# A decoder layer on one core: weights earlier, gate work on GpSimd, another order of side steps, and the 64-to-128 merge in two fours

## The chip, the cores and the metric

The kernel runs on one core of a Trainium2 chip. The time is what the device takes for one execution, in microseconds; the median of the runs counts. The engines are PE (TensorE, matrix products), DVE (VectorE), ACT (ScalarE), POOL (GpSimd) and SP (SyncE, which issues the DMAs here). Each engine works off its own instructions in order, and waits for others by semaphores.

## The reference

One layer on x of 256 x 2048 (float32), with two branches side by side:

```python
shift, scale, gate = split(silu(c) @ w_ada + b_ada)
h = rms_norm(x, norm_pre_w) * (1 + scale) + shift
proj = h @ w_in                    # all branch inputs and the two merge gates
q, k, v = conv_silu(gdn_qkv)       # 16 q/k heads, 32 value heads, width 128
o_a = gated_delta_rule(l2(q), l2(k), v, g_log, beta)     # needs (I + lower)^-1 for each head
y_a = (rms_norm(o_a) * silu(gdn_z)) @ w_proj_gdn
h_b = mlstm(conv_silu(ml_qk), ml_v, i, f)                # 8 heads
y_b = (sigmoid(ml_o) * rms_norm(h_b) * silu(ml_z)) @ w_proj_mlstm
x + gate * rms_norm((sigmoid(gate_a) * y_a + sigmoid(gate_b) * y_b) @ w_out)
```

## The kernel before

Every large product is made of three products of split operands: a weight tile `raw` (128 x 2048, 1 MB) is loaded by SP, ACT rounds it to `whi`, DVE or POOL subtracts to get `wlo` (in halves of 1024 columns, "pieces" below; four buffers each, three of `raw`), and PE multiplies both with `h_hi` and `h_lo`. `Stream` runs these pieces: it prepares up to three pieces ahead of the one that PE uses. `split_w` deals the subtraction out between POOL and DVE by a share (`START_SHARE`, then `LAST_SHARE` in the last start block, then 0).

Stages: the conditioning products with `ar` tiles (`ada`, DVE) run beside the first blocks of the start, in which 14 groups of 512 output columns (`START`: gates and value inputs) are summed over 16 chunks of `h` in blocks of chunks (`BLOCKS`); `part` holds the sums. Then eight GDN periods, `gdn_period(zg)`: each streams the projections of an even pair of heads, of z, and of an odd pair, and the work on the heads runs as "side" generators that advance by one step for each half piece or piece of the stream: `gdn_stage1` for each pair (convolution, SP's load `gb` of the decay rows, POOL's mask `dd`, ACT's exponentials, products `psa`, `psb`, `psv`), then for the four heads `base_inverse` (32 x 32 blocks are inverted on DVE in `xx`, whose input comes through DRAM by `ud` and `ug` and whose result goes back by `xd` and `xcmp`), then `gdn_stage2` (the blocks are merged: `mp` and `mx` from 32 to 64, `mq` and `mz` from 64 to 128; then `pa`, `pb`, `pc`, `po`), and the output transposes `pt<-con,on` with ACT's copies `oT`. Then the mLSTM heads in the same manner, and the projections `py` and `pw`.

What sets the order is the program: steps of the generators are written between pieces of the stream. `Side` keeps a `debt` of DVE's extra work; each step pays off `STEP_US`, and `room` holds a generator back while the debt is high. `banks` and `free` hold it back until PSUM tiles are free. What one engine gets is then in its queue in that order, DMAs on SP included.

```python
def step(self):
    self.t += 1
    self.debt = max(0.0, self.debt - STEP_US)
    for e in list(self.gens):
        if next(e[1], self) is self:
            self.gens.remove(e)
```

Of the kernel before, what the change touches and what calls it, by code (L numbers as in the profile page):

```python
# [25 lines left out]
LAST_SHARE = 0.3  # L26
STEP_US = 2.1
# [90 lines left out]
def hybrid_layer_kernel(  # L118
# [150 lines left out]
    crow = sp.tile([P, D], F32, name="crow", tag="ar", bufs=ADA_BUFS)[0:1]  # L269
    SP.dma_start(crow, c_row)  # L270
# [5 lines left out]
    A.activation(crow, crow, AF.Silu)  # L276
    for q in range(4):
        T.matmul(csil[:, q * 512:(q + 1) * 512], one_row, crow[:, q * 512:(q + 1) * 512], start=True, stop=True)
# [28 lines left out]
    def x_chunks(k0, k1):  # L307

        x_scale(k0)
        for k in range(k0, k1, 2):  # L310
            if k + 2 < k1:
                x_scale(k + 2)
            x_turn(k)
    x_chunks(0, 6)
# [10 lines left out]
    def h_chunk(k):  # L325
# [6 lines left out]
        split(hf, h_hi[:, k], h_lo[:, k], G)  # L332
# [11 lines left out]
    def ada_units():  # L344

        adders = []
        for k in range(KC):
            for pt in range(2):
                def prep(h, raw, k=k, pt=pt):
                    V.scalar_tensor_tensor(raw, raw, 1.0, csil, op0=ALU.mult, op1=ALU.mult,  # L350
                                           accum_out=ad[:, pt * KC + k:pt * KC + k + 1])
                    if 4 <= 2 * k + pt < 8:
                        j = 2 * (2 * k + pt)
                        if j > 8:
                            x_turn(j)
                        if j < 14:
                            x_scale(j + 2)
                    h_chunks(k - 1)
                    if pt == 1:
                        due.append(k)  # L360
                        if k == 0:
                            h_chunks(0)
                            x_chunks(6, 10)
                        elif k == KC - 1:
                            banks_open()
# [7 lines left out]
    def banks_open():  # L373

        nonlocal pg
        pcs.close()
        pg = ctx.enter_context(tc.tile_pool(name="pg", bufs=4, space=PSUM))
        share[1] = LAST_SHARE

    def branches_open():  # L380
# [3 lines left out]
        share[1] = 0.0  # L384
# [8 lines left out]
    def add_start_groups(bi):  # L393
        k0, nk = BLOCKS[bi]
        lastb = bi == len(BLOCKS) - 1
        adders, parts_ = [], []
        for g in range(len(START)):
            st_ = {}

            def use(h, hi, lo, g=g, st_=st_):  # L400
                if h == 0:
                    st_["ps"] = [jtile(f"pn{i}") for i in range(2)]
                for kc in range(min(2, nk - 2 * h)):
                    kr = h * 2 + kc
                    k = k0 + kr
                    h_chunks(k)
                    o = kc * 512
                    for b in range(2):
                        mm3(st_["ps"][b], h_hi[:, k, b * P:(b + 1) * P], h_lo[:, k, b * P:(b + 1) * P],
                            hi[:, o:o + 512], lo[:, o:o + 512], kr == 0, kr == nk - 1)  # L410

            def after(g=g, st_=st_):
                for b in range(2):
                    if bi == 0:
                        A.copy(part[g][:, b], st_["ps"][b])
                    else:
                        V.tensor_tensor(part[g][:, b], st_["ps"][b], part[g][:, b], op=ALU.add)  # L417
                if bi == len(BLOCKS) - 2 and g == 3:
                    late_consts()
                if lastb:  # L420
                    pt = part[g].rearrange("p b c -> p (b c)")
                    A.activation(pt, pt, AF.Silu if g in (9, 11, 13) else AF.Sigmoid)
                    if g < 8:
                        SP.dma_start(gate_dr[g], part[g])
                    elif g % 2:
                        V.tensor_tensor(part[g], part[g], part[g - 1], op=ALU.mult)
                        SP.dma_start(gate_dr[8 + (g - 8) // 2], part[g])
                    if g == NG - 1:
                        branches_open()
            parts_.append((w_in[START[g]][:, k0 * 512:(k0 + nk) * 512], use, after))  # L430
        if nk == 2:
            for g in range(0, NG, 2):
                def use2(h, hi, lo, g=g):
                    parts_[g + h][1](0, hi, lo)
                    parts_[g + h][2]()
                adders.append(lambda g=g, use2=use2:
                              stream.add((parts_[g][0], parts_[g + 1][0]), prep_w, use2))
        else:
            for src, use, after in parts_:
                adders.append(lambda src=src, use=use, after=after:  # L440
                              stream.add(src, lambda h, raw: prep_w(h, raw, nk * 512), use, (nk + 1) // 2, after))
# [3 lines left out]
    def gates(ps):  # L445
# [15 lines left out]
        V.tensor_scalar(u, e, 1.0, None, op0=ALU.add)  # L461
# [4 lines left out]
        V.tensor_scalar(u, u, -1.0, None, op0=ALU.add)  # L466
        V.tensor_tensor(e, e, u, op=ALU.subtract)
        V.tensor_tensor(e, e, r, op=ALU.mult)
        V.tensor_tensor(l, l, e, op=ALU.add)
        mn, sp_ = ab, u  # L470
        V.scalar_tensor_tensor(mn, xb, 0.0, l, op0=ALU.min, op1=ALU.subtract)
        V.scalar_tensor_tensor(sp_, xb, 0.0, l, op0=ALU.max, op1=ALU.add)
# [865 lines left out]
```

## Time and profile before

| | us |
|---|---|
| median of 3 runs (1624.42 to 1629.12) | 1628.48 |
| the profiled execution | 1630.52 |
| its span | 1628.7 |
| PE busy | 1589.6 |
| DVE, ACT, POOL busy | 1130.8, 935.9, 266.2 |

The granted clock of PE was 0.998 on average, and the DMAs moved 372.37 MB. In the lines shown below, L223 is the line of all split products, L169 and L170 those of the rounding and the subtraction, so tiles are told apart by name. The number in brackets at a row's end is idle time before the instruction, with what ended it.

### The profile page before, as it was taken

The page shows a single profiled execution, that of the slowest core. Times are in us where ns is not written, and L with a number is a line of the kernel's source. Part 1 is how long each engine was busy: PE and PEld are TensorE (multiplying, and loading weights), DVE is VectorE, ACT ScalarE, POOL GpSimd, SP SyncE. Part 2 cuts the span into 40 slices and gives each one's busy share as a digit, 9 for nine tenths or more (in the row PEclk, how much of TensorE's full clock was granted, in tenths as well). Part 3 has the DMA queues.
Part 4 walks back from the last instruction along what each step waited for, and adds up shares of the span by engine and source line. Part 5 has one row for each costly group of instructions (what it writes and reads, how often), then busy time and mean ns, then how long its engine had stood idle before and what let it go on. Part 6 is the DMA issues. An engine that isn't in the chain of part 4 may idle for free.

```text
span 1628.7 us, 25437 instructions
## 1 busy us (share of the span) xinstructions
PE 1589.6 (98%) x9844; PEld 1388.5 (85%) x9844; DVE 1130.8 (69%) x1784; ACT 935.9 (57%) x1494; POOL 266.2 (16%) x200
## 2 busy tenths in 40 slices
PE   6999999999999999999999999999999999999998
PEld 4888888789998999999898989789987788888886
DVE  5586555665678797969696969686777556756654
ACT  7744446564655666666666666665565544444442
POOL 3877762220000010000000000000100000100100
PEclk9999999999999999999999999999999999999999
DMA  9998775665455555555546464657888668766573
GB/s 375 381 363 327 274 280 181 240 246 206 163 182 166 181 178 191 173 177 173 183 164 196 162 198 168 185 177 257 289 312 303 211 236 298 275 239 245 201 271 118
DMA packets 96259, 372.37 MB, mean 229 GB/s; under 512 B 26261, under 2 KB 46213, under 8 KB 58249
## 3 DMA queue, kind: packets, MB, share of 16 engines
q1 hardware_dynamic: 96138, 370.75, 64.8%
q8 instruction: 77, 1.26, 0.3%
q14 instruction: 44, 0.36, 0.1%
HBM read 354.40 MB, written 16.31 MB: 228 GB/s over the span
## 4 chain that ended last, share of the span: by engine, by line
PE 66%; DVE 7%; ACT 4%; DMA 3%; issue 2%; POOL 1%; SPq 0%; DVEq 0%; POOLq 0%; ACTq 0%
PE pt L223 24%; PE py L223 15%; PE pn L223 14%; PE pw L223 5%; DVE wlo L170 3%; ACT whi L169 2%; DMA raw<-in_dram 1%; DMA ya<-o_dr 1%; PE psa L223 1%; DVE mqk L579 1%; DVE part L417 1%; DVE gacc L1034 1%; PE mq L777 1%; PE mz L785 1%; PE pt L859 0%
## 5 line engine op out<-in xcount | busy, mean ns | idle before, releaser
L170 DVE TENSOR_TENSOR wlo<-raw,whi 128x1024 fp32r<-128x1024 f32 x439 | 545.1, 1250 | 267.6 <-ACT whi L169 261.7
L169 ACT CAST whi<-raw 128x1024 fp32r<-128x1024 f32 x514 | 531.2, 1051 | 301.7 <-PE pn L223 142.9
L223 PE MATMUL pt<-h_hi,whi 128*128 128x256 f32 x1280 | 368.2, 288 | 0.2 <-ACT sz L877 0.2
L223 PE MATMUL pt<-h_hi,wlo 128*128 128x256 f32 x1280 | 362.4, 283 | 1.5 <-DVE wlo L170 1.5
L223 PE MATMUL pt<-h_lo,whi 128*128 128x256 f32 x1280 | 362.0, 283 | 0.0
L223 PE MATMUL pn<-whi,h_hi 128*128 128x512 f32 x896 | 353.9, 395 | 3.7 <-ACT whi L169 2.9
L223 PE MATMUL pn<-wlo,h_hi 128*128 128x512 f32 x896 | 351.0, 392 | 5.4 <-POOL wlo L170 4.1
L223 PE MATMUL pn<-whi,h_lo 128*128 128x512 f32 x896 | 350.2, 391 | 0.0
L223 PEld LDWEIGHTS pt<-h_hi,wlo 128*128 128x128 f32 x1280 | 245.1, 192 | 2.1 <-DVE wlo L170 2.1
L223 PEld LDWEIGHTS pt<-h_hi,whi 128*128 128x128 f32 x1280 | 245.3, 192 | 1.7 <-ACT sz L877 0.4
L223 PEld LDWEIGHTS pt<-h_lo,whi 128*128 128x128 f32 x1280 | 245.3, 192 | 0.2
L223 PEld LDWEIGHTS pn<-wlo,h_hi 128*128 128x128 f32 x896 | 168.8, 188 | 43.4 <-POOL wlo L170 6.6
L223 PEld LDWEIGHTS pn<-whi,h_hi 128*128 128x128 f32 x896 | 168.7, 188 | 40.3 <-ACT whi L169 3.3
L170 POOL TENSOR_TENSOR wlo<-raw,whi 128x1024 fp32r<-128x1024 f32 x75 | 180.4, 2413 | 126.1 <-ACT whi L169 113.0
L223 PEld LDWEIGHTS pn<-whi,h_lo 128*128 128x128 f32 x896 | 168.7, 188 | 35.7 <-POOL h_lo L170 0.3
L223 PE MATMUL py<-whi,yhi 128*128 128x512 f32 x384 | 150.9, 393 | 2.8 <-ACT vt L965 2.8
L223 PE MATMUL py<-whi,ylo 128*128 128x512 f32 x384 | 149.8, 390 | 0.0
L223 PE MATMUL py<-wlo,yhi 128*128 128x512 f32 x384 | 149.7, 390 | 0.0
L417 DVE TENSOR_TENSOR part<-pn,part 128x512 f32<-128x512 f32 x112 | 74.0, 686 | 50.5 <-PE pn L223 50.5
L169 ACT CAST yhi<-ya 128x512 fp32r<-128x512 f32 x48 | 29.9, 622 | 129.9 <-PE py L223 125.6
L170 DVE TENSOR_TENSOR ylo<-ya,yhi 128x512 fp32r<-128x512 f32 x48 | 33.2, 692 | 94.1 <-ACT yhi L169 92.2
L579 DVE SCALAR_TENSOR_TENSOR qs<-pt,gcv,qs 128x255 f32<-128x255 f32 (+2 forms) x192 | 92.1, 480 | 4.6
(242 smaller groups left out, 1787.7 us busy)
## 6 DMA issues: line engine op xcount, KB each, us to landing
raw<-in_dram SPq DMA_DIRECT2D x259, 1024.0 KB
ar<-in_dram SPq DMA_DIRECT2D x32, 1024.0 KB
raw<-in_dram SPq DMA_DIRECT2D x28, 512.0 KB
ya<-o_dr SPq DMA_DIRECT2D x32, 256.0 KB
gate_dr<-part SPq DMA_DIRECT2D x11, 512.0 KB
gb<-rows SPq DMA_DIRECT2D x20, 256.0 KB
ug<-ud SPq DMA_DIRECT2D x32, 128.0 KB
o_dr<-oT SPq DMA_DIRECT2D x16, 256.0 KB
```

Source lines behind the costliest of these rows:

```text
L169: A.copy(hi, src)
L170: (eng or V).tensor_tensor(lo, src, hi.bitcast(F32), op=ALU.subtract)
L223: T.matmul(ps, l, r, start=start and i == 0, stop=stop and i == 2, skip_group_check=True)
L417: V.tensor_tensor(part[g][:, b], st_["ps"][b], part[g][:, b], op=ALU.add)
L579: V.scalar_tensor_tensor(dst[:, n, sh:], src[:, 0:S - sh], taps(n, 3 - sh), dst[:, n, sh:], op0=ALU.mult, op1=ALU.add)
L777: T.matmul(psp[64:128, m * 64:(m + 1) * 64], um(m)[0:64, 64:128], y0[:, m], start=True, stop=True)
L785: T.matmul(psz[0:64, m * 64:(m + 1) * 64], p2[64:128, m], x0[64:128, m, 64:128], start=True, stop=True)
L1034: V.scalar_tensor_tensor(gate_half[q], raw[:, q * 1024:(q + 1) * 1024], sil[:, i:i + 1], gate_half[q], op0=ALU.mult, op1=ALU.add)
```

## The change

It alters the following. The conditioning vector is loaded into two `part` tiles, so that the first weights follow two `ar` loads; the start blocks become seven, in which the first six groups begin with one chunk, and the stream prepares one piece ahead in the first of them. The gate arithmetic goes from DVE to POOL with more steps between, POOL also multiplies the gate parts, and the share of POOL in the last start block becomes 0. The step budget goes from 2.1 to 1.6 us, and the steps that hold PE long take something off the debt. The start of `gdn_stage2` is tied to a step count. The output transposes wait for four free tiles instead of two. In the mLSTM heads mask and exponentials are issued within the convolution, and the scores wait for the seventh GDN application. In the merge from 64 to 128, eight `mq` and eight `mz` become four first products, then four second products in turn with the other four first ones, then the last four second ones, all in one PSUM tile `mqz`.

```diff
-LAST_SHARE = 0.3
-STEP_US = 2.1
+STAGE2_STEPS = 32
+STEP_US = 1.6
...
-    crow = sp.tile([P, D], F32, name="crow", tag="ar", bufs=ADA_BUFS)[0:1]
-    SP.dma_start(crow, c_row)
+    crow = [part[4 + i].rearrange("p b c -> p (b c)")[0:1] for i in range(2)]
+    for i in range(2):
+        SP.dma_start(crow[i], c_row[:, i * 1024:(i + 1) * 1024])
...
-    stream = Stream(load_w, side)
-    BLOCKS = ((0, 2), (2, 2), (4, 4), (8, 4), (12, 4))
-    PACE = (4, 9.5, 16.5, 26, 32, 32)
+    stream = Stream(load_w, side, 2)
+    NG, NE = len(START), 6
+    EARLY, REST, ALL = range(NE), range(NE, NG), range(NG)
+    BLOCKS = ((EARLY, 0, 1, 1.1, 3.5), (REST, 0, 2, 4, 8), (EARLY, 1, 3, 8, 12), (REST, 2, 2, 12, 16.5),
+              (ALL, 4, 4, 16.5, 26), (ALL, 8, 4, 26, 32), (ALL, 12, 4, 32, 32))
...
-        share[1] = LAST_SHARE
+        share[1] = 0.0
...
+                stream.ahead = 3 if bi else 1
...
-                        V.tensor_tensor(part[g], part[g], part[g - 1], op=ALU.mult)
+                    G.tensor_tensor(part[g], part[g], part[g - 1], op=ALU.mult)
...
-        V.tensor_scalar(u, e, 1.0, None, op0=ALU.add)
+        G.tensor_scalar(u, e, 1.0, None, op0=ALU.add)
...
+        res["t"] = side.t
         psa = gtile("psa", True)
...
+        side.debt -= 1.6
...
-        yield from wait(1)
+        yield
+        while zg < 7 and side.t < res["t"] + STAGE2_STEPS - 1:
+            yield
         side.add(gdn_stage2(zg, res, zr), 0)
...
-        psp = gtile("mq", True)
-        for m in range(8):
-            T.matmul(psp[64:128, m * 64:(m + 1) * 64], um(m)[0:64, 64:128], y0[:, m], start=True, stop=True)
...
-        psz = gtile("mz", True)
-        for m in range(8):
-            T.matmul(psz[0:64, m * 64:(m + 1) * 64], p2[64:128, m], x0[64:128, m, 64:128], start=True, stop=True)
...
+        psq = psz = gtile("mqz", True)
...
+        for i in range(3):
+            side.debt -= 0.5
+            first, second = slice(4 * i, 4 * i + 4), slice(4 * i - 4, 4 * i)
+            for m in range(4 * i, 4 * i + 4):
+                if i > 0:
+                    T.matmul(psz[0:64, (m - 4) * 64:(m - 3) * 64], p2[64:128, m - 4], x0[64:128, m - 4, 64:128],
+                             start=True, stop=True)
+                if i < 2:
+                    T.matmul(psq[64:128, m * 64:(m + 1) * 64], um(m)[0:64, 64:128], y0[:, m], start=True, stop=True)
...
+        applied[0] += 1
...
-        yield from free(2)
+        yield from free(4)
...
-        yield from conv_silu(ps, lambda n, j: late_c["mcv"][:, (m * 4 + n) * 4 + j:(m * 4 + n) * 4 + j + 1], qk)
...
-        ee = decay_mask(gb)
-        yield
-        decay_exp(ee, gb, av[0], av[0], av[1])
-        yield from wait(8 if m == 0 else 1)
...
+        for i, _ in enumerate(conv):
+            if i == 1:
+                ee = decay_mask(gb)
+            elif i == 3:
+                decay_exp(ee, gb, av[0], av[0], av[1])
+            yield
+        yield
+        while applied[0] < 7:
+            yield
```

Three places in the order of instructions, each as it stands before and after.

SP's queue in one GDN period, from the even pair's `gb` to the next `ud` and `ug`. Before:

```order
L597 DMA gb<-rows 128x512
L164 DMA raw<-in_dram 128x2048 x6
L597 DMA gb<-rows 128x512
L164 DMA raw<-in_dram 128x2048 x2
L720 DMA xd<-xx 128x8x32
L723 DMA xcmp<-xd 32x1x256 x4
L164 DMA raw<-in_dram 128x2048
L864 DMA o_dr<-oT 128x2x256 x2
L164 DMA raw<-in_dram 128x2048
L689 DMA ud<-au 32x4x32 x8
L693 DMA ug<-ud 32x1x1024 x4
```

The same stretch of SP's queue after the change:

```order
L603 DMA gb<-rows 128x512
L164 DMA raw<-in_dram 128x2048 x6
L728 DMA xd<-xx 128x8x32
L731 DMA xcmp<-xd 32x1x256 x4
L603 DMA gb<-rows 128x512
L164 DMA raw<-in_dram 128x2048 x4
L888 DMA o_dr<-oT 128x2x256 x2
L697 DMA ud<-au 32x4x32 x8
L701 DMA ug<-ud 32x1x1024 x4
```

`xd` and `xcmp` moved ahead of the odd pair's `gb`, and past two `raw`. So it stands in six of the eight periods (zg 1 to 6).

SP's queue at the start, from the small constants on (`ar` are the conditioning weights, `raw` those of the projections). Before:

```order
L157 DMA npre<-in_dram 128x16
L322 DMA ar<-in_dram 128x2048 x4
L164 DMA raw<-in_dram 128x1024 x2
L322 DMA ar<-in_dram 128x2048
L164 DMA raw<-in_dram 128x1024 x2
```

And after the change:

```order
L157 DMA npre<-in_dram 128x16
L322 DMA ar<-in_dram 128x2048 x2
L164 DMA raw<-in_dram 128x512 x4
L322 DMA ar<-in_dram 128x2048
L164 DMA raw<-in_dram 128x512 x2
```

The first weights stand behind two `ar` instead of four, in loads of half the size.

ACT's queue around the last mLSTM head (`mqk` is the silu of its convolution, `dd` the exponentials, `vt` the copies of its values, `gr` a copy for the output gate). Before:

```order
L582 ACTIVATE mqk<-mqk 128x1024
L169 CAST yhi<-ya 128x512
L169 CAST whi<-raw 128x1024 x2
L612 ACT_TABLE_LOAD
L612 ACTIVATE dd<-dd,tt 128x128
L613 ACTIVATE dd<-gb,tt 128x128
L614 ACTIVATE dd<-dd,tt 128x128
...
L1047 COPY gr<-gps 1x512
L169 CAST yhi<-ya 128x512
L169 CAST whi<-raw 128x1024
L965 COPY vt<-pn_12708 128x2x256
```

And after:

```order
L618 ACT_TABLE_LOAD
L618 ACTIVATE dd<-dd,tt 128x128
L619 ACTIVATE dd<-gb,tt 128x128
L620 ACTIVATE dd<-dd,tt 128x128
...
L169 CAST whi<-raw 128x1024 x2
L588 ACT_TABLE_LOAD
L588 ACTIVATE mqk<-mqk 128x1024
L169 CAST yhi<-ya 128x512
L169 CAST whi<-raw 128x1024 x2
L1077 COPY gr<-gps 1x512
L169 CAST yhi<-ya 128x512
```

The six exponentials moved ahead of the silu; between the silu and `vt` none stand now.

More of the change, by code (lines that the diff above doesn't have):

```diff
@@ L393, in add_start_groups @@
     def add_start_groups(bi):
-        k0, nk = BLOCKS[bi]
+        groups, k0, nk = BLOCKS[bi][:3]
         lastb = bi == len(BLOCKS) - 1
-        adders, parts_ = [], []
-        for g in range(len(START)):
-            st_ = {}
[L400 to L425, printed above, removed]
-                        V.tensor_tensor(part[g], part[g], part[g - 1], op=ALU.mult)
[L427 to L441, printed above, removed]
+        def use(g, ps, c, hi, lo, o):
+            k = k0 + c
+            h_chunks(k)
+            for b in range(2):
+                mm3(ps[b], h_hi[:, k, b * P:(b + 1) * P], h_lo[:, k, b * P:(b + 1) * P],
+                    hi[:, o:o + 512], lo[:, o:o + 512], c == 0, c == nk - 1)
@@ L519, in hybrid_layer_kernel @@
     ada = ada_units()
-    NG = len(START)
     ia = 0
-    for bi, (k0, nk) in enumerate(BLOCKS):
+    for bi, (groups, k0, nk, first, last) in enumerate(BLOCKS):
         if bi == len(BLOCKS) - 1:
@@ L526, in hybrid_layer_kernel @@
         for j, f in enumerate(fs):
-            ahead = PACE[bi] + (PACE[bi + 1] - PACE[bi]) * j / len(fs)
+            ahead = first + (last - first) * j / len(fs)
             while ia < len(ada) and ia < ahead:
@@ L794, in gdn_stage2 @@
         pa = gtile("pa", True)
+        side.debt -= 0.8
         for g, z, h, c in heads:
@@ L801, in gdn_stage2 @@
         pb = gtile("pb", True)
+        side.debt -= 0.8
         for g, z, h, c in heads:
```

104 lines of the change are left out of this document (73 added, 31 removed).

## Prediction

> **What bounds the kernel.** I read the engine totals first, then 40-us windows, then the table of waits, and last the timelines of the places that the waits name.
>
> ```profile
> PE 1589.6 (98%) x9844; PEld 1388.5 (85%) x9844; DVE 1130.8 (69%) x1784; ACT 935.9 (57%) x1494; POOL 266.2 (16%) x200
> ```
> ```profile
> 0.00:40.00 40.00, 27.72 (x85) 17.43 (x86) 21.87 (x27) 29.79 (x54) 11.88 (x11) 1.00 0.94 374
> 280.00:320.00 40.00, 35.39 (x152) 27.24 (x151) 27.57 (x36) 24.39 (x26) 9.66 (x4) 1.00 0.62 216
> 1240.00:1280.00 40.00, 37.18 (x147) 26.05 (x147) 23.59 (x28) 22.67 (x45) 1.85 (x3) 0.96 0.64 232
> ```
>
> The window rows give the stretch and its length, the busy us of PE, weight load, DVE, ACT and POOL, the granted clock, the DMA share and GB/s. TensorE (PE) is busy 1589.6 of 1628.7 us. All gaps together are 39 us, and the change adds or removes next to no multiplications: it can win only gaps, and it loses wherever it opens one. The windows show where gaps lie: 12.3 us at the start, 4.6 us in the last start block, 2.8 us in the mLSTM stage.
>
> **The change part by part.** Each sum is in us of PE's time. Gains first.
>
> Start (rows of a timeline: start, duration, engine, line, operation, out<-in, shape, count, and in brackets the idle time before it with what ended it). With only two `ar` tiles ahead of the first weights, the weights leave SP before the third `ar`, which had to wait for its buffer.
>
> ```profile
> 4.09 11.08 SPq L322 DMA_DIRECT2D ar<-in_dram  x4
> 14.95 2.29 DVE L350 SCALAR_TENSOR_TENSOR ar<-ar,csil 128x2048 f32<-128x2048 f32 x1
> 18.33 0.40 ACT L169 CAST h_hi<-hf 128x256 fp32r<-128x256 f32 x1
> 22.95 1.04 ACT L169 CAST whi<-raw 128x1024 fp32r<-128x1024 f32 x1 [1.11 <-DMA raw<-in_dram]
> 24.05 0.80 PE L223 MATMUL pn<-whi,h_hi 128*128 128x512 f32 x1 [2.88 <-ACT whi L169]
> ```
>
> Now the second `ad` sum (14.95 + 2.29) is last, `h_hi` follows at 18.33 to 18.73, and `whi` takes 1.04: the first product can come at 19.8 instead of 24.05, 4.25 earlier. The new block looks only one piece ahead, so the copies of the first four `part` stand in ACT before the fourth `whi`; they wait for products, and POOL's low half (2.4, row below) follows. I put two holes of about 1.2 and 0.8 against the gain. Taken: 2.2, ends 1.0 and 4.2.
>
> Last start block (rows of waits: who waits <- what ended it: us in all, times, longest).
>
> ```profile
> PE pn L223 <- POOL wlo L170: 4.1, 5, 1.2
> PE tp L501 <- ACT work L492: 1.1, 1, 1.1
> PE pn L223 <- DVE part L417: 0.8, 1, 0.8
> ```
> ```profile
> 301.13 1.06 ACT L422 ACTIVATE part<-part 128x1024 f32<-128x1024 f32 x1 [2.49 <-DVE part L417]
> 307.90 1.06 ACT L422 ACTIVATE part<-part 128x1024 f32<-128x1024 f32 x1 [3.82 <-DVE part L417]
> ```
> ```profile
> 303.20 2.38 POOL L170 TENSOR_TENSOR wlo<-raw,whi 128x1024 fp32r<-128x1024 f32 x1 [6.89 <-ACT whi L169]
> ```
>
> Between two groups a loop closes: sigmoid, two `whi`, POOL's `wlo` of 2.38, sums, sigmoid, 6.77 us (301.13 to 307.90). PE needs 24 products of 0.233 (35.39 / 152 in the window), so 5.6. With a share of 0 DVE makes every `wlo` and POOL's 2.38 leaves the loop. The three waits sum to 6.0. Taken: 5, since the gate arithmetic that goes to POOL and the added yields must not open a new one; ends 3 and 6.0.
>
> Step budget 2.1 to 1.6, with credits.
>
> ```profile
> PE pt L223 <- DVE wlo L170: 1.5, 3, 1.0
> PE psa L223 <- DVE ql L629: 1.3, 1, 1.3
> ```
>
> These are the waits of the first GDN transition (498 to 520), where DVE's side work is in front of `wlo` and `ql`. Taken: 1.5 of 2.8, as the same DVE work only moves later; ends 0 and 2.8.
>
> Output transposes (`free(2)` to `free(4)`).
>
> ```profile
> PE pt L859 <- ACT oT L862: 3.9, 5, 0.8
> ```
> ```profile
> 690.72 0.60 PE L859 MATMUL pt<-con,on 128*128 128x128 f32 x4
> 692.09 0.66 PE L859 MATMUL pt<-con,on 128*128 128x128 f32 x4 [0.78 <-ACT oT L862]
> ```
>
> The second four wait for ACT to empty the bank; with two free tiles they need not. They now come two pieces later. Taken: 3.9; ends 0 and 3.9.
>
> Merge in two fours, eight times.
>
> ```profile
> 706.01 0.39 PE L223 MATMUL pn<-whi,h_lo 128*128 128x512 f32 x1
> 706.33 0.69 PE L753 MATMUL mp<-ycmp,au 32*32 32x32 f32 x32
> 706.95 0.39 PE L223 MATMUL pt<-h_hi,whi 128*128 128x256 f32 x1
> ```
> ```profile
> 713.70 1.14 PE L777 MATMUL mq<-y,au 64*64 64x64 f32 x16
> ```
>
> Before, two insertions of 16 records each. A record of `mq` takes 58 ns ((1.14 - 0.22) / 16). In `mp`, where neighbours lie in other rows and columns of the array, 32 records fit between 706.33 and 706.95. If the alternating eight overlap as much, they take 0.53 instead of 0.93, 0.40 saved. The third insertion costs an entry (706.33 - 706.01 less 0.23, 0.09) and, as an estimate, twice that at its exit and restart: 0.28. Net 0.1 each, 0.8 taken; without overlap a loss of 2.2. `pa` still has a whole piece between it and the second `x0` copy that it waits for.
> The Trainium skill, TensorEngine Tiling (Array Packing), section Restrictions and Gotchas, speaks against this: different row tiles cannot access the same PSUM bank at one time. `mqz` is one bank, fed from rows 0 to 63 and from rows 64 to 127 in turn, while `mp` used two banks; no run here shows one bank. By that rule the term would be a loss of 2.2 and the forecast 3 us higher.
>
> mLSTM: mask and exponentials move into the convolution.
>
> ```profile
> 1041.78 0.24 PE L763 MATMUL mx<-pcm,xcmp 32*32 32x32 f32 x2 [1.20 <-ACT pcm L757]
> ```
> ```profile
> 1258.45 0.40 PE L223 MATMUL py<-whi,ylo 128*128 128x512 f32 x1
> 1261.67 0.50 PE L223 MATMUL py<-whi,yhi 128*128 128x512 f32 x1 [2.82 <-ACT vt L965]
> ```
> ```profile
> 1258.50:1261.60 3.10, 0.34 (x2) 0.00 (x0) 1.12 (x2) 3.10 (x8) 0.00 (x0) 1.00 0.93 347
> 1263.20:1266.60 3.40, 3.40 (x7) 1.29 (x7) 1.35 (x2) 1.32 (x2) 0.00 (x0) 0.51 0.12 48
> ...
> 1041.70:1046.00 4.30, 4.07 (x64) 3.13 (x65) 1.74 (x2) 3.62 (x7) 0.00 (x0) 1.00 0.35 97
> ```
>
> ACT is full there (3.10 of 3.10) with six exponentials and what stands behind them, and `vt` is late. The second window shows the after-effect: 3.4 us at a granted clock of 0.51 after a gap of 2.82, so 3.40 x 0.49 = 1.7 more. Behind the gap of 1.20 at 1041.78 the clock stays at 1.00 (third window). Taken: 4.5 of 1.20 + 2.82 + 1.7; ends 0 and 5.7.
>
> Gains together: 2.2 + 5 + 1.5 + 3.9 + 0.8 + 4.5 = 17.9.
>
> Now what the new order costs. `base_inverse` ends earlier, so in six GDN periods `xd` and the four `xcmp` stand in SP's queue ahead of the odd pair's `gb`, and no longer two `raw` behind it.
>
> ```profile
> 675.54 0.38 SPq L597 DMA_DIRECT2D gb<-rows  x1
> 680.96 7.38 SPq L164 DMA_DIRECT2D raw<-in_dram  x2
> 688.39 0.43 SPq L720 DMA_DIRECT2D xd<-xx  x1
> 693.80 2.76 SPq L723 DMA_DIRECT2D xcmp<-xd  x4
> ```
>
> SP waits for `xd` to land before it issues `xcmp`: 5.41 from 688.39 to 693.80, then 2.76. DVE's last `xx` moves four `wlo` ahead.
>
> ```profile
> 684.84 0.42 DVE L715 TENSOR_REDUCE xx<-tmp 128x8 f32<-128x256 f32 x1
> ```
>
> Two `wlo` belong to a `raw`, and two `raw` are 7 apart (680.96, 7.38 for both), so the last `xx` ends at 685.3 - 14 = 671.3, and SP sends `xd` at 675.5, right behind a `raw` as now, and `gb` goes at 675.5 + 5.4 + 2.8 = 683.7, 8.2 late. Who waits for it:
>
> ```profile
> 680.82 1.05 POOL L604 TENSOR_SCALAR_AFFINE_SELECT dd<-gb 128x256 f32<-128x256 f32 x2 [10.64 <-DMA gb<-rows]
> ```
> ```profile
> 681.50 0.40 ACT L612 ACTIVATE dd<-dd,ngt 128x128 f32<-128x128 f32 x1 [1.12 <-POOL dd L604]
> 684.23 1.57 ACT L573 ACTIVATE qs<-pt,gcv 128x256 f32<-128x256 f32 x4
> 685.65 2.02 ACT L169 CAST whi<-raw 128x1024 fp32r<-128x1024 f32 x2
> ```
> ```profile
> 686.76 1.23 DVE L170 TENSOR_TENSOR wlo<-raw,whi 128x1024 fp32r<-128x1024 f32 x1 [1.50 <-ACT whi L169]
> ```
>
> POOL's mask, then ACT's exponentials, and in ACT's queue behind them two squares, four `qs` scalings and the next `whi`; DVE's `wlo` follows and ends 6.5 after the first exponential (686.76 + 1.23 - 681.50). PE has three finished pieces at that point, to 690.72, where the transposes no longer stand: it needs that `wlo` at 690.95, so the exponentials have to begin by 684.45, 2.95 later than now. `gb` took 5.28 from issue to mask with a `raw` of 1 MB right ahead of it (680.82 - 675.54); that takes 2.6 (1049 KB at 374 / 0.94 KB/us, the first window) and was issued 0.4 earlier, so `gb` alone takes 3.1. So mask at 686.8, exponentials at 687.5, and PE stands for 3.05. Ends: 2.3, if the mask starts sooner, and 5.2, if `gb` alone takes 5.28 too. The half clock behind a gap of 2.82 costs 1.7, behind one of 1.2 nothing; 3.05 is nearest to the first, but the place was seen once, so I take half, 0.9. Six times 3.95 is 23.7.
> The Trainium skill, TensorE: Matmul & The Clock Gate, section Part 1, lets the clock fall after an idle window of about 3.4 us. The row shows it after 2.82, so the trace does not bear out so long a gap. By that rule the term is 6 x 3.05 = 18.3 and the forecast 5 us lower.
>
> **Sum.** -17.9 + 23.7 = +5.8. The profiled execution took 1630.5 (span 1628.7), so it would become 1636.3; it lay 2.0 above the median of the three runs, 1628.5, and from that the forecast is 1634.
>
> **Rivals.**
> - The late `gb` costs nothing, because ACT and DVE are a piece further ahead at that point than now (the point that decides: exponentials at 684.45 or earlier, measured from PE's position). For it: ACT and POOL are idle ahead of that chain now (1.12 and 10.64 in the rows), so neither has arrears to work off. Against it: the number of `whi` and `wlo` buffers stays at four. Time 1628.5 - 17.9 = 1610.6, faster. Chance 0.24.
> - `gb` costs its 3.05 but the clock holds, and the gains reach their upper ends, 23.4: 1628.5 + 18.3 - 23.4 = 1623.4. Chance 0.16.
> - `gb` alone is as slow as with a `raw` ahead: 5.2 + 1.7 each, 41.4 in all, against 17.9: 1652. Chance 0.08.
> - The change does not do what it says where the waits are: each removed wait uncovers the next and half of the gains stay, 9: 1628.5 + 23.7 - 9 = 1643. Chance 0.14.
>
> **Numbers.** The forecast has the other 0.38, between 1630 and 1639. Three runs of this kernel can tell about 0.3%, 4.9 us. Faster than 1623.6: 0.24 and two thirds of the second rival, 0.35. Slower than 1633.4: two thirds of the forecast's case, the last two rivals less 0.02, 0.45. The rest is 0.20. The range 1610 to 1650 leaves out half of the first rival and most of the third; the likeliest case alone has 1627 to 1641.
>
> **What would show it.** In the profile after: `gb` issued about 8 us behind its `raw` in six periods; POOL's mask about 6 later against `psa`; PE idle there 3 us, released by DVE `wlo`, with windows of granted clock near 0.5 behind. No PE wait on `oT`, on POOL `wlo` around 300, or on `vt` at 1260. First `pn` near 20. The alternating `mqz` at 0.5 or at 0.9. The prediction is wrong if PE runs through the six places, or if the waits there end on something other than `gb`'s chain.

## The result, and the profile after

| | before | after |
|---|---|---|
| median, us (4 runs each) | 1628.8 (1624.42 to 1630.52) | 1696.35 (1693.62 to 1699.41) |
| ratio to before, 95% interval | | 1.0419 [1.0401, 1.0437] |
| span of the profiled execution, us | 1628.7 | 1694.3 |
| mean granted clock of PE | 0.998 | 0.983 |

The change makes the kernel 67.6 us slower. The forecast was 1634 with a range to 1650: slower, and by much more than said. The engine totals of the profile after:

```profile
PE 1608.7 (95%) x9844; PEld 1398.1 (83%) x9844; DVE 1142.5 (67%) x1792; ACT 935.3 (55%) x1512; POOL 244.6 (14%) x197
```

The span grew by 65.6. PE has the same 9844 records, is busy 19.1 longer and stands idle 46.5 longer. ACT has the work that it had, and DVE is busy 11.7 longer. So PE waits, and runs slower behind the waits. The windows (stretch, its length, busy us of PE, weight load, DVE, ACT and POOL, granted clock, DMA share, GB/s) show the first two stretches of the prediction, and one of the GDN stage:

```profile
0.00:40.00 40.00, 27.04 (x84) 17.48 (x85) 19.48 (x27) 27.73 (x48) 10.45 (x9) 1.00 0.95 377
280.00:320.00 40.00, 36.90 (x151) 28.35 (x150) 25.41 (x34) 25.20 (x28) 2.17 (x6) 0.96 0.59 214
680.00:720.00 40.00, 34.62 (x200) 30.15 (x200) 26.18 (x52) 22.53 (x37) 3.26 (x5) 0.91 0.49 148
```

In the GDN window PE is idle 5.4 of 40 and its clock falls to 0.91. The table of waits names two tiles that it did not have in that place before (the `pn` that waits for ACT had 2.9 in one, at the start; `pa` had none):

```profile
PE pn L223 <- ACT whi L169: 37.5, 9, 5.5
PE pa L815 <- ACT x L800: 12.8, 7, 3.8
```

**One place in full.** SP's queue at the second of the six places, then the odd pair's mask on POOL, ACT from the first exponential, DVE's next `wlo`, and PE:

```profile
687.91 0.43 SPq L728 DMA_DIRECT2D xd<-xx  x1
693.37 2.76 SPq L731 DMA_DIRECT2D xcmp<-xd  x4
696.23 0.39 SPq L603 DMA_DIRECT2D gb<-rows  x1
696.71 0.38 SPq L164 DMA_DIRECT2D raw<-in_dram  x1
```
```profile
701.42 0.77 POOL L610 TENSOR_SCALAR_AFFINE_SELECT dd<-gb 128x256 f32<-128x256 f32 x2 [17.58 <-DMA gb<-rows]
```
```profile
701.86 0.40 ACT L618 ACTIVATE dd<-dd,ngt 128x128 f32<-128x128 f32 x1 [9.91 <-POOL dd L610]
```
```profile
707.02 1.22 DVE L170 TENSOR_TENSOR wlo<-raw,whi 128x1024 fp32r<-128x1024 f32 x1 [12.04 <-ACT whi L169]
```
```profile
701.73 0.39 PE L223 MATMUL pn<-whi,h_lo 128*128 128x512 f32 x1
707.04 0.80 PE L223 MATMUL pn<-whi,h_hi 128*128 128x512 f32 x1 [4.92 <-ACT whi L169]
708.30 0.80 PE L223 MATMUL pn<-wlo,h_hi 128*128 128x512 f32 x1 [0.46 <-DVE wlo L170]
```
```profile
708.30:711.00 2.70, 2.70 (x6) 2.15 (x7) 2.60 (x10) 2.63 (x5) 0.70 (x1) 0.50 0.69 185
711.00:714.00 3.00, 3.00 (x13) 2.46 (x12) 2.92 (x7) 2.28 (x4) 0.00 (x0) 0.90 0.45 188
```

Read from the top: SP waits 5.46 for `xd` to land, issues `xcmp`, and sends `gb` only then, with the next `raw` 0.48 behind it. 5.19 later POOL makes the mask, 0.44 later ACT begins the exponentials, and 5.16 behind them DVE begins its `wlo`. PE begins two products between 701.73 and 708.30 where it could have begun 6.57 / 0.228 of them, so 6.1 are lost. Then it runs at a granted clock of 0.50 and of 0.90: 2.70 x 0.50 + 3.00 x 0.10 = 1.65. Together 7.8. PE's first wait there ends on ACT's `whi`; the prediction had named DVE's `wlo`, the next link of the same chain.

**PE's progress.** All kernels have the same 8112 products of split operands, in the same order once the start blocks are over, so the start of the n-th one in two traces tells how far one is behind the other. After less before, in us, with the gain or loss between two rows, and what the prediction had for it:

| products | where | change of the lag | predicted |
|---|---|---|---|
| 0 to 480 | start | +2.7 | -2.2 |
| 480 to 1080 | further start blocks | 0.0 | 0 |
| 1080 to 1560 | last start block | +3.2 | -5 |
| 2400 to 3000 | first transition | -4.4 | -1.5 |
| 3000 to 5520, six stretches with the odd `gb` | GDN | +9.6, 6.8, 7.2, 6.5, 6.8, 10.6 = +47.4 | +23.7, less the output transposes' 3.9 |
| the stretches between them | GDN, `pa` | +14.9 | -0.8 |
| 5520 to the end | mLSTM and projections | +1.9 | -4.5 |
| sum | | +65.6 | +5.8 |

Two entries hold more than their name says: the last of the six stretches has the first mLSTM head in it, and the row of 5520 to the end has -4.7 at products 6480 to 6600, most of which the change did not bring (both below).

### The profile page after: what moved, and what is told of

It is laid out like the page before. It is cut to its first block, busy times and chain, and to the rows that moved or that the text cites. A ratio compares the mean times of both kernels' runs of the same rounds, so it can differ in the third digit from the quotient of the medians.

```text
span 1694.3 us, 25471 instructions
## 1 busy us (share of the span) xinstructions
PE 1608.7 (95%) x9844; PEld 1398.1 (83%) x9844; DVE 1142.5 (67%) x1792; ACT 935.3 (55%) x1512; POOL 244.6 (14%) x197
## 5 line engine op out<-in xcount | busy, mean ns | idle before, releaser
L170 DVE TENSOR_TENSOR wlo<-raw,whi 128x1024 fp32r<-128x1024 f32 x451 | 559.9, 1251 | 320.1 <-ACT whi L169 315.1
L169 ACT CAST whi<-raw 128x1024 fp32r<-128x1024 f32 (+1 forms) x517 | 530.9, 1045 | 296.9 <-PE pn L223 130.7
L223 PE MATMUL pn<-whi,h_hi 128*128 128x512 f32 x896 | 360.8, 403 | 39.9 <-ACT whi L169 37.5
L223 PE MATMUL pn<-wlo,h_hi 128*128 128x512 f32 x896 | 358.0, 400 | 10.8 <-DVE wlo L170 9.6
L223 PE MATMUL pn<-whi,h_lo 128*128 128x512 f32 x896 | 355.0, 396 | 0.7 <-DVE h_lo L170 0.7
L223 PEld LDWEIGHTS pn<-whi,h_hi 128*128 128x128 f32 x896 | 172.3, 192 | 81.8 <-ACT whi L169 41.2
L223 PEld LDWEIGHTS pn<-wlo,h_hi 128*128 128x128 f32 x896 | 172.1, 192 | 53.9 <-DVE wlo L170 17.9
L170 POOL TENSOR_TENSOR wlo<-raw,whi 128x1024 fp32r<-128x1024 f32 (+1 forms) x66 | 153.1, 2329 | 63.9 <-ACT whi L169 63.9
```

The lines of the kernel that those rows point to most:

```text
L169: A.copy(hi, src)
L170: (eng or V).tensor_tensor(lo, src, hi.bitcast(F32), op=ALU.subtract)
L223: T.matmul(ps, l, r, start=start and i == 0, stop=stop and i == 2, skip_group_check=True)
```

## Experiments

All times are medians, each with the kernel before on the same chip (1628.9 to 1630.5).

### The order on SP, and the merge: four kernels that undo the change step by step

In the first, `xd` waits until the odd pair's `gb` is issued:

```diff
     def decay_rows(row0):
+        gbs[0] += 1
...
+        while zg < 7 and gbs[0] < 2 * zg + 4:
+            yield
```

> The changed kernel, with xd held back until the odd pair's gb is issued, in all six periods; nothing else moved. Queue theory (SP waits for xd to land before xcmp and so sends gb 8 us late): the six holes at the fourth pn piece go; each cost 6.8 us of PE's progress and ate the 0.9 us that the output transposes gained, so 46 us come back: 1650. The holes before pa (3.3 to 3.8 us in three periods) stay. Rival (DVE's side work or the credits make the pieces late, gb is only the last to arrive): the holes stay or move to DVE wlo, 1685 to 1697.

Measured: 1657.41, ratio 1.0166 [1.0141, 1.019]. The change without that order is 38.9 us faster, 6.5 for each of six places (40.7 if each of the two is compared with its own runs of the kernel before). I had expected 46. At the first five places the lag now changes by -1.0 to +0.8; the sixth has the first mLSTM head beside it and keeps +6.7 (below). `pa` still waits, as expected:

```profile
PE pa L820 <- ACT x L805: 13.5, 6, 3.8
```

In the second, the merge goes back to eight `mq` and eight `mz`, with two credits instead of three:

```diff
-        for i in range(3):
-            side.debt -= 0.5
...
+        psp = gtile("mq", True)
...
+        side.debt -= 0.5
+        yield
...
+        psz = gtile("mz", True)
...
+        side.debt -= 0.5
+        yield
```

> The changed kernel with the merge of before (eight mq, eight mz, credit 0.5 us each, 1.0 us in two steps instead of 1.5 us in three). The order then has gb ahead of xd in all six periods. Queue theory and merge theory (the holes before pa come because the last x0 copy of the merge in fours stands behind the even pair's exponentials): both kinds of hole go, 46 and 15 us: about 1635. Rival (the holes before pa come from the late gb of the even pair alone): they stay, about 1650.

Measured: 1641.12, ratio 1.0068 [1.0044, 1.0093]. Here `gb` is ahead of `xd` without the hold of the first kernel, and no wait of `pa` is left, so the merge theory holds; the time is 6 above it. The third differs from it only in the two credits, 0.75 each, so that they sum to the 1.5 of the change:

> As the run with the old merge, but its two credits are 0.75 us each, so that the sum is 1.5 us as in the merge in fours. Same instructions; the order has xd ahead of gb in five of the six periods again. Queue theory: five holes of 7.7 us, 38 us on top of the run with the old merge, about 1673. Rival (the merge's own instructions cost the time): as the run with the old merge, about 1635.

Measured: 1684.67, ratio 1.033 [1.0309, 1.035], 43.6 more with the same instructions. The order turned in six periods, not in five. SP's queue and POOL's mask at the same place, first with credits of 0.5, then with 0.75:

```profile
679.91 0.38 SPq L603 DMA_DIRECT2D gb<-rows  x1
680.34 0.42 SPq L728 DMA_DIRECT2D xd<-xx  x1
685.81 2.76 SPq L731 DMA_DIRECT2D xcmp<-xd  x4
```
```profile
685.12 2.21 POOL L610 TENSOR_SCALAR_AFFINE_SELECT dd<-gb 128x256 f32<-128x256 f32 x2 [9.55 <-DMA gb<-rows]
```
```profile
686.93 0.43 SPq L728 DMA_DIRECT2D xd<-xx  x1
692.33 2.75 SPq L731 DMA_DIRECT2D xcmp<-xd  x4
695.18 0.39 SPq L603 DMA_DIRECT2D gb<-rows  x1
```
```profile
700.28 0.77 POOL L610 TENSOR_SCALAR_AFFINE_SELECT dd<-gb 128x256 f32<-128x256 f32 x2 [17.42 <-DMA gb<-rows]
```

From issue to mask `gb` takes 5.21 behind a `raw` issued 0.42 earlier and 5.10 behind small loads. It took 5.28 before and 5.19 after. But nowhere here is `gb` alone: where no `raw` stands right ahead of it, the next one follows 0.5 behind. The packets in the traces tell the two apart. In the six places before, where a `raw` is ahead, the first of `gb`'s 128 packets starts 3.5 to 3.6 behind the issue, and the last ends at 4.6 to 4.9. After, the first starts at 1.0 to 1.3, but the last still ends at 4.6 to 4.8, among the packets of the `raw` behind. One `gb` of the profile after, that of the first mLSTM head, has no `raw` within 4.5 us on either side (SP's queue, then two windows):

```profile
1076.56 0.32 SPq L603 DMA_DIRECT2D gb<-rows  x1
1081.11 0.33 SPq L164 DMA_DIRECT2D raw<-in_dram  x1
```
```profile
1077.51:1079.27 1.76, 0.00 (x0) 0.00 (x0) 0.00 (x0) 1.76 (x5) 0.00 (x0) 0.50 0.44 149
1079.27:1081.10 1.83, 0.80 (x1) 0.29 (x1) 1.25 (x2) 1.80 (x4) 0.00 (x0) 0.50 0.00 0
```

Its 256 KB move in these 1.76 us (149 GB/s), and then the DMAs rest: it has landed 2.71 behind its issue. With the 0.4 to 0.5 from landing to mask in the six places, that is the 3.1 of the prediction. So the figure was right for a `gb` alone, and the prediction missed the `raw` behind it. No run moved that `raw`, so this rests on the traces only.

The waits of PE on ACT's `whi` go from 10.2 to 41.6:

```profile
PE pn L223 <- ACT whi L169: 10.2, 3, 5.6
```
```profile
PE pn L223 <- ACT whi L169: 41.6, 9, 6.4
```

In this kernel the lag grows by at most 0.6 between the six places and by 6.9 to 11.6 in them, so the time is lost there. At the place shown SP's queue differs from that of the second kernel in this order alone and PE's not at all; some of DVE's inversion steps stand a few `wlo` elsewhere as well. It also shows what turned the order: half a microsecond of credit, which lets `base_inverse` end a step earlier.

The fourth puts the start back too (the GDN and mLSTM parts stay):

> The kernel before with the changes from the GDN periods on alone (step budget, credits, step count, four free tiles, mLSTM exponentials) and the old merge: start blocks, gates and POOL share as before. By PE's progress the change lost 2.7 us in the first 100 us and 3.2 us in the last start block, and won 6 us at the first GDN transition, 4.7 at the output transposes, 2 to 5 in the mLSTM stage: 1628.8 - 13 to 16 = 1613 to 1616. Rival (the GDN side has another loss beside the two kinds of hole): 1620 or more.

Measured: 1635.12, ratio 1.0033 [1.002, 1.0046]: a miss. The parts that were to win 9.9 lose 5 or so, and the rival, another loss on the GDN side, is right.

The ladder so far: 1696.4 less 38.9 (order) less 16.3 (merge) less 6.0 (start) is 1635.1, and 5 to 6 remain for the other parts.

### The merge by itself

Two kernels have the merge in fours alone, put into the kernel before. The first of them had kept one credit of 0.8 at `pa` from the change, which its expectation does not name:

> The kernel before with the merge in two fours alone, no credit; gb stays ahead of xd. The changed kernel's records show four alternating pairs in the time of four single products, so PE's work is 0.2 us a period less, 1.4 in all. pa comes one piece later and waits for an x0 copy behind the even pair's exponentials, which begin 4.2 us after psa here: holes of 0.3 to 0.8 us in six periods. Together 1629 to 1634. Rival (the merge itself is what costs, as the title of the change has it): holes of 3 us and half clock behind them, 1645 or more.

Measured: 1639.22, ratio 1.0059 [1.0045, 1.0072], between the two theories. The second is without that credit:

> The merge in fours alone, now with no change of the debt anywhere (the earlier run of the merge alone also took 0.8 us off the debt at pa, which moves the po step). Theory: the loss comes from the second copy into x0, which in most periods stands in ACT's queue behind the even pair's six exponentials, so PE waits for it at pa as before: 5 to 10 us in all, 1634 to 1639 us. Rival: the credit at pa did it, and the merge by itself costs nothing: 1628 to 1630, no wait of pa.

Measured: 1644.53, ratio 1.0086 [1.0069, 1.0104]. The credit was not the cause; without it the loss is larger, and above what I expected, near the 16.3 of the ladder. The largest gaps of PE in its GDN periods are 3.17 and 1.84 ahead of `pa`, and 2.14 ahead of the second products:

```profile
PE pa L801 <- ACT x L787: 5.9, 3, 3.2
PE mqz L782 <- ACT p L789: 2.1, 1, 2.1
```

The cause stands in ACT's queue. Here is the change itself: the even pair's `gb` is issued, its mask comes late, and the copy into `x` that `pa` needs stands behind all of it (SP, ACT, PE):

```profile
730.89 0.43 SPq L603 DMA_DIRECT2D gb<-rows  x1
```
```profile
743.55 0.40 ACT L618 ACTIVATE dd<-dd,ngt 128x128 f32<-128x128 f32 x1 [5.38 <-POOL dd L610]
...
747.40 0.36 ACT L800 COPY x<-mqz 64x256 f32<-64x256 f32 x1
```
```profile
740.76 0.67 PE L795 MATMUL mqz<-x,p 64*64 64x64 f32 x8
747.82 1.16 PE L815 MATMUL pa<-rr,x 128*128 128x128 f32 x8 [3.31 <-ACT x L800]
```

The products that the copy waits for were begun at 740.76, but ACT is held by the exponentials, which wait for the mask, until 743.55. The third kernel moves `pa` one step back:

```diff
+        yield
         yield from banks(1)
         pa = gtile("pa", True)
```

> The same merge in fours with pa one step later, so that the second copy into x0 has half a piece more. Theory (the wait of pa is the whole loss): the sum of pa's waits falls from 8.4 to under 3, and the time to 1628 to 1632. Rival (the loss lies in the order of the rest, since everything behind pa shifts by a step as well): 1635 or more.

Measured: 1635.76, ratio 1.0041 [1.0027, 1.0056]. No wait of `pa` is left, and 8.8 us come back. The merge still loses 6: other waits are there instead, at `po`, at the first `mqz`, at the output transposes.

```profile
PE pt L865 <- ACT oT L868: 4.7, 6, 0.8
PE po L828 <- ACT ys L819: 4.5, 3, 1.5
```

So the time is the rival's (1635 or more), though the waits that the theory names are gone. They were 8.8 of the 15; one step more shifts everything behind it as well, and what makes up the last 6 was not taken apart.

### The start

The start alone, in the kernel before:

> The kernel before with the start part alone: conditioning vector in part tiles, seven start blocks, one piece ahead in the first, POOL's share 0 in the last block, gate arithmetic and gate products on POOL; from the GDN periods on as before. By PE's progress this part lost 5.8 us in the changed kernel (2.7 in the first 110 us, 3.2 from there to 375 us), though the first product came 4.3 us earlier: 1636. Rival (that loss came with the later step budget): 1624 to 1630.

Measured: 1636.23, ratio 1.0035 [1.0022, 1.0048], as expected. Then the same start with two pieces ahead instead of one, and the product of the gate parts on DVE as before:

```diff
-                    G.tensor_tensor(part[g], part[g], part[g - 1], op=ALU.mult)
+                    V.tensor_tensor(part[g], part[g], part[g - 1], op=ALU.mult)
-                stream.ahead = 3 if bi else 1
+                stream.ahead = 3 if bi else 2
```

> The start part alone, with two pieces ahead in the first block instead of one, and the three gate products on DVE as before instead of POOL; the two act at different places. If one piece ahead costs the holes at 30 to 36 us (ACT's fourth whi behind eight copies), PE's progress at 140 us is no longer 2.0 behind the kernel before but 1 to 2 ahead; if POOL's product slows DVE's wlo beside it (2.5 instead of 1.2 us at 337), the holes of 1.4 us at 340 and 352 go and the last block loses 0 to 1 instead of 3.1. Both: 1630 to 1632. Rival (half-size loads or the block split cost it): 1636 as before.

Measured: 1627.85, ratio 0.9991 [0.9981, 1.0001], better than expected: 8.4 less than the start as changed. PE's lag behind before is -0.5 at product 480 (with one piece ahead +2.0) and -0.9 at 1560 (+5.2). With one piece ahead, ACT makes eight copies into `part` tiles before the fourth `whi` (first row); with two ahead it makes four, and the `whi` comes at 25.81 (second):

```profile
29.14 1.05 ACT L169 CAST whi<-raw 128x1024 fp32r<-128x1024 f32 x1
```
```profile
25.81 1.05 ACT L169 CAST whi<-raw 128x1024 fp32r<-128x1024 f32 x1
```

In the last start block it is POOL's product beside DVE's `wlo` (after; POOL, and DVE beside it and without it):

```profile
336.02 2.40 POOL L422 TENSOR_TENSOR part<-part,part 128x1024 f32<-128x1024 f32 x1 [53.77 <-ACT part L418]
```
```profile
336.91 3.73 DVE L170 TENSOR_TENSOR wlo<-raw,whi 128x1024 fp32r<-128x1024 f32 x2 [2.07 <-ACT whi L169]
331.28 2.36 DVE L170 TENSOR_TENSOR wlo<-raw,whi 128x1024 fp32r<-128x1024 f32 x2 [2.07 <-ACT whi L169]
```

Two `wlo` take 3.73 beside it and 2.36 alone. If the first stands until POOL's product ends at 338.42, they end at 338.42 + 2.36 = 340.78; they end at 340.64. The Trainium skill, SBUF — State Buffer, section SBUF: two separate sides, says that a DVE instruction with two SBUF inputs and a GpSimd one that reads SBUF lock each other out for a whole instruction. By this the first `wlo` loses 1.5; the trace agrees, with 1.4. But taking the product away brings no gain in this block either (-0.4 from 1080 to 1560, where the prediction has -5). PE's waits there, after and with the product on DVE:

```profile
PE pn L223 <- DVE wlo L170: 4.3, 6, 1.3
```
```profile
PE pn L223 <- DVE wlo L170: 2.1, 4, 0.8
```

The wait on POOL's `wlo` (4.1 before) is gone, and DVE, which makes every `wlo` now, is what PE waits for.

### The GDN and mLSTM parts

Four free tiles at the output transposes, and the early mask and exponentials for the mLSTM heads but the first:

```diff
-        yield from free(2)
+        yield from free(4)
...
+            if m > 0 and i == 1:
+                ee = decay_mask(gb)
+            elif m > 0 and i == 3:
+                decay_exp(ee, gb, av[0], av[0], av[1])
```

> The kernel before with two parts: four free tiles for the output transposes, and mask and exponentials within the convolution for the second to fourth mLSTM head only (the first head's wait for the one mask buffer held ACT for 8 us in the run with the start of before). Five waits on oT go, 4.7 us, and the wait on vt with the half clock behind it, 4.5: 1630.5 - 9 = 1621. Rival (each uncovers the next wait, as with DVE's qs in the run with the start of before): 1626 to 1631.

Measured: 1632.48, ratio 1.0021 [1.001, 1.0033]: a miss. The rival is nearer, and the time lies above its 1631 too. The waits on `oT` are gone, and others have come, above all:

```profile
PE pc L812 <- DVE rr L806: 3.2, 4, 0.9
```

With the step budget of 1.6 and the credits added, but in force only until the first `base_inverse` has ended:

> As the run with two parts, and the step budget of 1.6 us with its credits until the first base_inverse ends, 2.1 us and no credits behind it. The first GDN transition gave 6.1 us in every run with that budget, later periods lost 1 to 2 us each to DVE's qs and ql: 1621 - 5 = 1616. Rival (the gain of the transition is only borrowed from the periods behind it): 1621.

Measured: 1630.67, ratio 1.0007 [0.9996, 1.0018]: a miss, about 2 won by the medians and not 5. The early exponentials alone:

> The kernel before with mask and exponentials within the convolution for the second to fourth mLSTM head, and nothing else (two free tiles as before). The wait on vt and the half clock behind it gave 4.8 us at that place in the two runs that had this part, and 1.6 to 1.9 us were lost 30 us later to DVE's hn: 1629 - 3 = 1626. The run with four free tiles as well was 1632 (holes before pc, on DVE's rr); if these come from the four free tiles they are gone here. Rival (they come from the mLSTM part): 1630 or more.

Measured: 1631.01, ratio 1.0007 [0.9995, 1.0018]: the rival again. The waits of `pc` are not there, so they come with the four free tiles. Against the profiled execution of the kernel before, PE gains 4.8 at `vt` (products 6480 to 6600) and loses 2.0 at 5520 to 5640 and 1.8 behind 6600; at the end it is 0.2 ahead. But the five kernels that left the mLSTM heads as they were (two with the start alone, three with the merge alone) gain 3.8 to 4.1 at `vt` as well. ACT's first cast of `ya`, the input of the output projections, before and in the start with two pieces ahead, then PE's wait on `vt` in the latter:

```profile
1253.51 0.62 ACT L169 CAST yhi<-ya 128x512 fp32r<-128x512 f32 x1 [4.25 <-DMA ya<-o_dr]
```
```profile
1251.01 0.62 ACT L169 CAST yhi<-ya 128x512 fp32r<-128x512 f32 x1 [1.84 <-DMA ya<-o_dr]
```
```profile
1259.17 0.50 PE L223 MATMUL py<-whi,yhi 128*128 128x512 f32 x1 [0.37 <-ACT vt L971]
```

In that one execution before, the load `ya` took 7.6 from its issue to this cast, and `vt` stood behind it in ACT's queue. In the five it took 5.1 to 5.4; PE waits 0.3 to 0.6 on `vt`, and its clock stays at 1.00. So most of the wait of 2.82, with its half clock, came from one late load, and 0.7 to 1.0 of the 4.8 is left for the exponentials. Why the load was late is not known.

And the budget with the early exponentials, but with `free(2)`:

> The run with three parts, with two free tiles instead of four: the small step budget with its credits until the first base_inverse ends, and the mLSTM part. 6.1 us at the first transition, 3 in the mLSTM stage, and of the 3.2 us lost in the next period what is not from the output transposes: 1629 - 6 to 9 = 1620 to 1623. Rival (the transition only borrows DVE time from the next period, whichever way the transposes go): 1626.

Measured: 1628.04, ratio 0.9989 [0.9978, 1.0001]: a miss of theory and rival. By the medians `free(4)` loses 2.6 where it was to win 3.9; the two intervals just overlap. Last, the kernel with the old start and merge, with the first mLSTM head's mask and exponentials where they were:

> The run with the old start, the new GDN and mLSTM parts and the old merge (1635.1 us), but with mask and exponentials of mLSTM head 0 behind the convolution as before. Theory: the 7.5 us lost there, less the 3.1 that came back, come from those exponentials standing in ACT ahead of whi while the mask waits for its turn; without them 1629.5 to 1631.5. Rival: the loss there comes from the later GDN work that the smaller step budget has pushed into that place, and nothing comes back: 1634 to 1636.

Measured: 1633.86, ratio 1.0024 [1.0012, 1.0036], against 1.0033 [1.002, 1.0046] with them early: between the theories, and not told apart by the times. The traces do tell it apart at the place. There (products 5280 to 5520) the lag grows by 7.5 with the early ones and by 3.1 without. With them the mask waits for a DVE product that comes late, and ACT's exponentials hold up what stands behind (POOL, then PE):

```profile
1035.22 0.77 POOL L605 TENSOR_SCALAR_AFFINE_SELECT dd<-gb 128x256 f32<-128x256 f32 x2 [14.46 <-DVE au L672]
```
```profile
1040.22 0.79 PE L224 MATMUL pn<-whi,h_hi 128*128 128x512 f32 x1 [3.18 <-ACT whi L170]
```

But behind that place the first gets 3.1 back and the second 0.2. So in these two executions the early exponentials of that head cost 1.5 net. The other 3 are there without them; the smaller step budget, which leaves more of the last GDN period's work for this place, would explain them, but it was not tried by itself.

### What is left when the parts that lose are taken away

The start with two pieces ahead, the step budget up to the first `base_inverse`, and the early exponentials of the later mLSTM heads; merge, output transposes and the rest as before:

> The start part with two pieces ahead and the gate products on DVE, together with the small step budget until the first base_inverse ends and the mLSTM exponentials of the second to fourth head; merge and free tiles as before. By PE's progress the first gave 0.9 us up to 375 us, the second 6.1 at the first transition, of which 2.7 to 3.7 are lost again in the two periods behind it: 1629.5 - 3.5 to 6 = 1623.5 to 1626, clear of the kernel before in five rounds. Rival (a gain ahead of the GDN periods is taken back at the next fixed wait): 1628 to 1630.

Measured: 1625.0, ratio 0.9963 [0.9948, 0.9977], 5 us faster than before, as expected. In the profiled execution PE is 2.3 ahead of before at product 1560 and 7.1 at 3000, and gives part of that back by the end (2.6).

## Why the prediction was right and wrong

The time lies 62 above the forecast: 15 from the six places, 17 from the merge, 13 from the start with the last start block, and 16 from the other parts.

- **The six places: right in mechanism, mis-sized.** The order, the chain and the count were as said. The sum had 3.95 for one: a hole of 3.05 and 0.9 for the clock. The place in full has 6.1 and 1.65. The step that failed is "so `gb` alone takes 3.1", with the mask that it gives at 686.8: the 3.1 is right for a `gb` alone, but in the new order the next `raw` is issued 0.5 behind it, and the mask comes 5.1 to 5.2 behind the issue. I had asked what stands ahead of `gb` and not what follows. Beside that, `gb` left 9 later against `psa` (4.3 to 5.4 ahead of it before, 4.0 to 4.4 behind it after), not 8.2. So the mask was 9 late, not 6. The third rival, "`gb` alone is as slow as with a `raw` ahead", with 41.4, came out in its price: the places cost 38.9 with the new merge and 43.6 with the old one. That it did is luck, since its reason was wrong. That rival gave 1652; the 44 us from there to 1696 are the merge (17), the start and the last start block (13) and the other parts (16), less 2.5 by which the places came cheaper.
- **The half clock.** I took half of 1.7, because a gap of 2.82 had been seen once. Behind a gap of 4.92 the clock is 0.50 for about 4 us. The Trainium skill, TensorE: Matmul & The Clock Gate, section Part 1, lets the clock fall after an idle window of about 3.4 us; the gap of 4.92 agrees with that, and so the rule's 18.3 for the term failed on the hole, not on the clock.
- **The merge.** I took 0.8 as a gain and the bank rule of the Trainium skill as its risk. Both were beside the point. The products do overlap in one bank:

```profile
735.61 0.22 PE L795 MATMUL mqz<-x,p 64*64 64x64 f32 x1
735.61 0.22 PE L798 MATMUL mqz<-y,au 64*64 64x64 f32 x1
735.66 0.22 PE L795 MATMUL mqz<-x,p 64*64 64x64 f32 x1
735.67 0.22 PE L798 MATMUL mqz<-y,au 64*64 64x64 f32 x1
```

  A pair begins every 58 ns, as one record did before, so the trace does not bear out that two row tiles cannot use one bank at a time (the Trainium skill, TensorEngine Tiling (Array Packing), Restrictions and Gotchas). The merge cost 15 to 16 us. The step that failed is "`pa` still has a whole piece between it and the second `x0` copy"; 8.8 came back when `pa` moved. I had looked at PE only. The copy stands in ACT's queue, and behind the even pair's exponentials.
- **Start and last start block.** The first product came at 19.8, as said. The holes behind it, which I put at 2.0, ate all 4.3 and 2.7 more, because one piece ahead leaves ACT's copies in front of the fourth `whi`. In the last block POOL's `wlo` left the loop, as said; DVE's took its place, and POOL's product slowed it. Of the 8.2 between -5 and +3.2 taking the product away gives back 3.5 (+3.2 with it, -0.4 without). The step "POOL's 2.38 leaves the loop" failed: I had taken the wait off without asking what DVE, with every `wlo`, would then need. I had put the low end at 3.
- **The first transition** won more than its 1.5: PE is 4.4 further at product 3000, of which about 2 are seen in the time.
- **Output transposes.** The wait went where I said (none on `oT`), and `pc` waits instead. The rival "each removed wait uncovers the next" held here, and it does not exclude the others; I had priced it as if it did.
- **mLSTM.** The wait of `py` on `vt` went as well, but the term of 4.5 was mis-sized: its 2.82 and 1.7 came mostly from one late load in the one execution that I had read, and five kernels with the old order wait 0.3 to 0.6 there. ACT had been idle 4.25 ahead of the cast in front of `vt`, which I had not looked at. What the early exponentials of the first head cost, the term did not have at all.

The chance of 0.45 for slower came from the six places alone. The sum was close to zero because two wrong terms, gains of 17.9 and losses of 23.7, nearly cancelled.

What stays open: how much `gb` gains when the `raw` behind it is moved, why the load `ya` came late in one execution, and which of the waits that came behind the later `pa` make up the last 6 us of the merge.

## What to carry to other kernels

A store and the load that reads it back, issued in order on one queue, hold up everything behind them for the round trip; look what stands there, since a planner's credit of half a microsecond far away can turn that order (43.6 us with the same instructions). Look at what follows a load too: here its last packets ran among those of the next load. Before a copy is called hidden, read what stands ahead of it in its own engine's queue, and what that waits for. Before a wait is priced, look for it in a second trace of the same code: one execution can have a late load of its own. Measure the parts of a large change one by one: three of these parts together, the start with two pieces ahead, are at 0.9963, and all of them as changed at 1.0419.

## What the runs showed of the hardware

- A load of 256 KB that spreads two rows to 128 partitions had landed 2.7 us behind its issue with no 1 MB load within 4.5 us of it, and 4.6 to 4.9 in the six places, with a 1 MB load issued 0.4 to 0.5 ahead or behind. A store of 8 x 32 to each partition kept the queue for 5.4 us before the load that reads it back could be issued.
- Two products in different rows of the array that write other partitions of one PSUM bank overlap in full: 58 ns for the pair, 58 ns for one.
- A subtraction on DVE with two inputs lost 1.4 us to a POOL product that still had 1.5 to run.
